# A hybrid encoder layer: a triangular substitution spread over the weight tiles, two projections exchanged, and one projection's sums in other PSUM banks

## The chip, the core and the metric

The kernel runs on one core of a Trainium2 chip. TensorE (PE) multiplies matrices and sums into PSUM banks of 128 partitions by 512 floats; VectorE (DVE), ScalarE (ACT) and GpSimd (POOL) do the rest, and SyncE (SP) issues most DMAs, some of which POOL issues too. Each engine works through its own list of instructions in order and waits where an instruction's operands or buffers aren't ready. The metric is the device time of one execution in microseconds (us), as the median of several runs.

## The reference

Two layers over 256 tokens of width 1024. Each layer normalises its input and feeds two mixers, whose outputs are gated, projected, merged and projected once more:

```python
h = rmsnorm(x, norm_w)
qa, ka, va, ab, za, qb, kb, vb, zb, ga, gb = split(h @ w_in)
# branch a: gated delta rule, chunks of 64, forward and backward
T = triangular_solve(I + L, I)            # L strictly lower, 64 x 64 for each head and chunk
u, w = T @ (v * beta), T @ (k * beta * exp(g))
ya = rmsnorm(o_fwd + o_bwd, gdn_norm_w) * silu(za)
# branch b: differential attention, 8 heads, two softmaxes per head
a = softmax(q0 @ k0.T) - lam * softmax(q1 @ k1.T)
yb = rmsnorm(a @ vb, subln_w) * (1 - lambda_init) * silu(zb)
# merge
x = x + (sigmoid(ga) * (ya @ w_pa) + sigmoid(gb) * (yb @ w_pb)) @ w_out
```

All inputs and the output are 32-bit floats; a final rmsnorm closes the trunk.

## The kernel before

A product of 32-bit precision is made of three matmuls: each operand is split into a high part and the rest, and high by high, high by low and low by high are summed in one bank. For the weights, SP loads a tile `raw` of two k-tiles (256 rows by 512 columns, a *weight pair*, three buffers), ACT casts it to `hi` (L248) and DVE subtracts to get `lo` (L250), two buffers of each. Twelve matmuls of 128x512 then use the pair: two k-tiles, two halves of the tokens, three products (L262 to L264). Their sums stand in two accumulators of a pool `ps_p` of four banks, which the next projection but one needs again. Smaller products use `ps_c` (two banks) and `ps_m` (two).

A layer goes through its projections in this order: the convolved q, k, v of branch a (`conv`) with q and k of branch b between (`qk_part`); `zb` and `za` in two halves each, with the eight heads' scores, softmaxes (`scores`) and value products (`attend`) woven in; the gates `gb`; `pb`, which multiplies the attention's output; the gates `ga`; `pa`; `o`. So zb0 means the first half of zb, of four weight pairs.

Beside them runs the triangular solve. `substitute` solves blocks of 32 by 32 on DVE, 31 rows, of which each takes a product (`fstmp`) and a subtraction (`X`). `spread_blocks` copies the result transposed (`lt`) and writes both to a DRAM tile `udr`; `merges(0)` and `merges(1)` read that back into `T64` tiles and `U_` (DMAs of POOL and SP) and join the blocks on PE to 64 (`y64p`) and 128 (`y128p`). `chunks(0)` and `chunks(1)` then apply the delta rule; the four products `ktm` by `kds` on DVE belong to them. Their result is scaled, turned (`pt_ya`) and split into `yaT`, which `pa` multiplies; `ybT`, from `pt_yb`, is the same for `pb`.

A scheduler sets each engine's list: it simulates the engines and takes the instructions by priority as they come ready. `tc.issue_after(x)`, here often as `behind(x)`, keeps an instruction behind x in the order, and `place(at)` names a matmul of a projection: `names[at // 8]`, k-tile `at % 8`, so that 32 to 39 is gb0. The steps of `merges` and `chunks` are pinned to such places. `mark[nm, kp]` holds cast and subtraction of weight pair kp.

The convolved v goes through DRAM to be turned (`bounce`, tile `tb_v`), and ACT scales it into `vtm` (L571). ACT also empties qk's accumulators into `stg` (L462).

Of the kernel before, what the change touches and what calls it, by code (L numbers as in the profile page):

```python
# [8 lines left out]
F32 = mybir.dt.float32  # L9
F32R = mybir.dt.float32r  # L10
I32 = mybir.dt.int32
AF = mybir.ActivationFunctionType
ALU = mybir.AluOpType
# [4 lines left out]
P = 128  # L18
# [3 lines left out]
NM = SEQ // P  # L22
# [6 lines left out]
HP = None  # L29
# [20 lines left out]
def hybrid_encoder(  # L50
# [31 lines left out]
    ps_c = pool("ps_c", 2, PSUM)  # L82
# [5 lines left out]

    def banks2(name):
        return [ps_p.tile([P, 512], F32, tag="p", name=f"{name}{i}") for i in range(2)]  # L90

    def bank_c(name):
        return ps_c.tile([P, 512], F32, tag="c", name=name)

    def mid(ap, n):
        return ap.unsqueeze(1).to_broadcast([ap.shape[0], n] + list(ap.shape[1:]))

    def last(ap, n):
        return ap.unsqueeze(ap.ndim).to_broadcast(list(ap.shape) + [n])

    mark = {}
# [119 lines left out]
    def behind(ins):  # L221
        return nullcontext() if ins is None else tc.issue_after(ins)
# [29 lines left out]
            for k in range(2):  # L252
                yield 2 * kp + k, hi[:, k, :n], lo[:, k, :n]

    def proj_tm(act, w, c0, n, evac, nm, places=(None,) * 4, spare=(), later=None, turned=(), between=None):

        accs = banks2(f"pp_{nm}")
        for kt, hi, lo in weights(w, c0, n, nm, places, later=later, spare=spare, turned=turned):
            for m in range(NM):
                ts_ = slice(m * P, (m + 1) * P)  # L260
                o = accs[m][:, :n]
                T.matmul(o, act[kt // 4][:, 0, kt % 4, ts_], hi, start=kt == 0, stop=False)  # L262
                T.matmul(o, act[kt // 4][:, 0, kt % 4, ts_], lo, start=False, stop=False)  # L263
                mark["proj"] = T.matmul(o, act[kt // 4][:, 1, kt % 4, ts_], hi, start=False,  # L264
                                        stop=kt == KT - 1).ins
                mark["done", nm, kt] = mark["proj"]
        if between:
            between()
        for m in range(NM):
            evac(m, accs[m][:, :n])  # L270
# [89 lines left out]
    for l in range(DEPTH):  # L360
# [175 lines left out]
        def conv(seg, c_base, slot, g):  # L536
            def evac_conv(acc, b0):
                vf = []
                for b in range(2):
                    j4 = b0 + b  # L540
                    cb = c_base // P + 4 * g + j4
                    ca = work.tile([P, SEQ], F32, tag="conv", name=f"cv{seg}{l}{g}{j4}", bufs=2)
                    S.activation(ca, acc[:, b, :], AF.Copy, scale=cw[:, 2, cb : cb + 1])  # L543
                    for j in (0, 1, 3, 4):
                        sft = j - 2
                        o0, o1 = max(0, -sft), SEQ - max(0, sft)
                        V.scalar_tensor_tensor(ca[:, o0:o1], acc[:, b, o0 + sft : o1 + sft],  # L547
                                               cw[:, j, cb : cb + 1], ca[:, o0:o1],
                                               ALU.mult, ALU.add)
                    if b == 0:  # L550
                        ths = work.tile([P, 2, SEQ], F32, tag="vf", name=f"th{seg}{l}{g}{j4}", bufs=2)
                    th = ths[:, b, :]
                    S.activation(th, ca, AF.Tanh, scale=0.5)
                    if slot is None:
                        f_ = th.rearrange("p (m t) -> p m t", m=NM)
                    else:
                        f_ = kq[:, 4 * g + j4, :, slot, :]
                    mark["conv"] = V.scalar_tensor_tensor(
                        f_, th.rearrange("p (m t) -> p m t", m=NM), 1.0,
                        ca.rearrange("p (m t) -> p m t", m=NM), ALU.add, ALU.mult).ins  # L560
                    vf.append(f_)
                if seg == "q":
                    return
                if seg == "v":
                    tb = squares(f"v{l}{g}{b0}")
                    turn_squares(tb, ths.rearrange("p b (m t) -> p (b m) t", m=NM))
                    bounce(tb, f"v{l}{g}{b0}")
                    for b in range(2):
                        for m in range(NM):
                            hd = 4 * g + b0 + b  # L570
                            S.activation(vtm[:, m, hd, :].rearrange("p (i d) -> p i d", i=4),  # L571
                                         tb[:, :, 2 * b + m, :], AF.Copy, scale=nrm[:, m, hd : hd + 1])
                    return
                pt = bank_c(f"ct{seg}{l}{g}{b0}")
                ptv = pt.rearrange("p (b m d) -> p b m d", b=2, m=NM)
                for b in range(2):
                    for m in range(NM):
                        T.transpose(ptv[:, b, m, :], vf[b][:, m, :], ident)
                bs = slice(4 * g + b0, 4 * g + b0 + 2)
                S.copy(ktm[:, :, bs, :].rearrange("p m b d -> p b m d"), ptv)  # L580
                for b in range(2):
                    for m in range(NM):
                        hd = 4 * g + b0 + b
                        S.activation(sqj[:, :P], ptv[:, b, m, :], AF.Square,
                                     accum_out=ssk[:, m, hd : hd + 1])
            proj_fm(hT, wl, c_base + 512 * g, evac_conv, f"{seg}{l}{g}",
                    turned=(3,) if (seg, g) == ("q", 1) else ())

        gdr = dram.tile([NM, 8, 2, P], F32, tag="gdr", name=f"gdr{l}")
        lnc = small.tile([P, 2, NM, NH], F32, tag="lnc", name=f"lnc{l}")  # L590
# [106 lines left out]
            with tc.issue_after(mark["conv"]):  # L697
                V.tensor_copy(la[64:P], lt[64:P].rearrange("p j i -> p i j"))

        def substitute(j0, j1):  # L700
            for j in range(j0, j1):
                ni, nr = 31 - j, j + 1
                tv = tmp[:, : nr * ni].rearrange("p (c i) -> p c i", c=nr)
                V.tensor_tensor(tv, mid(la[:, j, j + 1 :], nr), last(X[:, :nr, j], ni), ALU.mult)
                V.tensor_tensor(X[:, :nr, j + 1 :], X[:, :nr, j + 1 :], tv, ALU.subtract)

        def spread_blocks():
# [12 lines left out]
        def step(gens):  # L720

            for g_ in gens:
                next(g_)
# [86 lines left out]
        def chunks(g):  # L810
# [17 lines left out]
                S.copy(flat(y1[d]), ps)  # L828
            yield
            for d in range(2):  # L830
                with behind(mark["spread"]):
                    V.tensor_tensor(st[d], st[d], last(kds[:, d, hs4], P), ALU.mult)
                ps = four(f"sp{d}", lambda j: st[d][:, j, :], lambda j: y1[d][:, j, :])
                S.copy(flat(st[d]), ps)
# [52 lines left out]
        def scores(h, after):  # L887
            es = work.tile([P, 2, NM, SEQ], F32, tag="w4a", name=f"es{l}{h}", bufs=2)
            mx = small.tile([P, 2, NM], F32, tag="mx", name=f"mx{l}{h}")
            sp = [bank_c(f"sc{l}{h}{n}") for n in range(2)]  # L890
            for qt in range(NM):
                for n in (1, 0):
                    rows = slice(64 * n, 64 * n + 64)
# [45 lines left out]
        def z_part(z, c_base, nm, i):  # L939
            def evac_z(m, ps):  # L940
                silu2(z[i][:, m, :], ps)
            proj_tm(hT, wl, c_base + 512 * i, 512, evac_z, f"{nm}{l}{i}")


        if l == 0:
# [23 lines left out]
        conv("q", C_QA, 1, 1)  # L969
        take_blocks()  # L970
        qk_part(0, 1)
        substitute(0, 8)
        conv("v", C_VA, None, 0)
        qk_part(1, 0)
        substitute(8, 14)
        conv("v", C_VA, None, 1)
        qk_part(1, 1)
        substitute(14, 20)

        names = [f"{nm}{l}{i}" for nm in ("zb", "za", "gb", "pb", "ga") for i in range(2)]  # L980
        place = lambda at: mark["done", names[at // KT], at % KT]
        es = {}
        for p in range(4):
            z_part((zb, za)[p // 2], (C_ZB, C_ZA)[p // 2], ("zb", "za")[p // 2], p % 2)
            for h in (2 * p, 2 * p + 1):
                es[h] = scores(h, place(4 * h))
                if h:
                    attend(h - 1, es[h - 1], place(4 * h + 1), place(4 * h + 3))
            if p == 1:
                substitute(20, 31)  # L990
                spread_blocks()
                mg = [merges(0), merges(1)]
                step(mg)
                step(mg)
        def gated(o_, z_, r_, nw_, yT, nm, tiles=range(NM)):
            for i in range(2):
                for m in tiles:
# [35 lines left out]
        ybT = pair(f"ybT{l}")  # L1033
        gated(lambda i, m: heads4(ob[i][:, m, :]), zb, rb, nw[:, 1:2], ybT, f"yb{l}")

        branch(ybT, w_pb[l], gtb, f"pb{l}")
        gta = gate(C_GA, f"ga{l}", "eo")
        ch = [chunks(0), chunks(1)]

        def run(gen, at):  # L1040
# [1 line left out]
            with tc.high_priority(offset=HP):  # L1042
                next(gen, None)

        order = [(mg, 34), (mg[:1], 37), (mg[1:], 39), (mg, 42), (mg, 44)]
        order += [(ch[i : i + 1], at + i) for at in (48, 51, 54, 57, 60, 63, 66) for i in range(2)]
        for gens, at in order:
            if at == 48:
                key_sums()
            for gen in gens:  # L1050
                run(gen, at)
# [96 lines left out]
```

## Time and profile before

| | |
|---|---|
| median of three runs | 776.07 us (775.88 to 779.17) |
| profiled execution, its own time | 778.13 us |
| its span | 776.4 us |
| mean granted clock of TensorE | 0.994 |
| busy: PE, DVE, ACT, POOL | 752.7, 576.8, 471.7, 123.3 us |

The profile shows one execution, and its engine times are shares of its span. A row of a timeline is start, duration, engine, line, operation and its tiles (output<-input), and in brackets how long the engine was idle before and what ended that. A row of groups (with |) ends in the sum of busy time, the mean of one in ns, and the idle time before. A row of windows begins with the stretch and its length, then busy time and count of PE, PE's weight loads, DVE, ACT and POOL, the granted clock, the share of DMA time and GB/s. Buffer numbers are left out of names.

### The profile page before, as it was taken

The numbers are of one execution on the slowest core, as the hardware profiler recorded it, in microseconds if no ns is written. First come the engines' busy times: TensorE is split into PE (matmuls) and PEld (weight loads), VectorE is DVE, ScalarE is ACT, GpSimd is POOL, SyncE is SP. The second block draws the span as 40 slices with busy tenths as digits, with TensorE's granted clock in tenths as the row PEclk, the third lists the DMA queues.
The fourth block names the chain that finished last, engine by engine and source line by source line (L and its number), as shares of the span: only waits on it lengthen the run. The fifth ranks groups of instructions, "written<-read, shape, count | busy, mean of one in ns | idle before, by whom it ended". The sixth has DMA issues, their size and how long they took to land. (4 is left out here: it accounts for less than half of the span.)

```text
span 776.4 us, 13742 instructions
## 1 busy us (share of the span) xinstructions
PE 752.7 (97%) x5158; PEld 641.0 (83%) x5158; DVE 576.8 (74%) x1083; ACT 471.7 (61%) x1012; POOL 123.3 (16%) x187
## 2 busy tenths in 40 slices
PE   7999999989999999999999999999999998999996
PEld 4899889967778789888889889887777887998884
DVE  5686899989976735567677779999998575537682
ACT  6657675658776654565545678556687656456542
POOL 5000431111231020000010025202114012001000
PEclk9999999999999999999999999999999999999999
DMA  7752667755596523357674257767557862333641
GB/s 230 236 176 82 223 198 198 224 149 175 151 221 201 184 89 108 85 171 234 217 224 136 82 156 252 203 189 221 161 163 177 231 189 89 109 109 109 210 143 54
DMA packets 71794, 131.24 MB, mean 169 GB/s; under 512 B 12287, under 2 KB 12751, under 8 KB 71728
## 3 DMA queue, kind: packets, MB, share of 16 engines
q1 hardware_dynamic: 62718, 111.94, 48.3%
q0 software_dynamic: 6304, 15.15, 7.4%
q10 hardware_dynamic: 2706, 3.28, 1.2%
q8 instruction: 40, 0.66, 0.4%
q14 instruction: 26, 0.21, 0.1%
HBM read 123.44 MB, written 6.91 MB: 168 GB/s over the span
## 5 line engine op out<-in xcount | busy, mean ns | idle before, releaser
L263 PE MATMUL pp_qk<-lo_qk,hT 128*128 128x512 f32 x128 | 51.0, 399 | 0.8 <-DVE lo_qk L250 0.5
L264 PE MATMUL pp_qk<-hi_qk,hT 128*128 128x512 f32 x128 | 50.0, 391 | 0.0
L250 DVE TENSOR_TENSOR lo_qk<-raw_qk,hi_qk 128x1024 fp32r<-128x1024 f32 x32 | 39.7, 1242 | 9.8 <-ACT hi_qk L248 9.5
L262 PE MATMUL pp_qk<-hi_qk,hT 128*128 128x512 f32 x128 | 45.2, 393 | 0.0
L250 DVE TENSOR_TENSOR lo_pb<-raw_pb,hi_pb 128x1024 fp32r<-128x1024 f32 x16 | 19.6, 1224 | 32.4 <-ACT hi_pb L248 32.4
L904 ACT ACTIVATE es<-sc,mx 128x256 f32<-128x256 f32 x64 | 29.7, 476 | 21.4 <-DVE mx L902 21.4
L248 ACT CAST hi_qk<-raw_qk 128x1024 fp32r<-128x1024 f32 x28 | 29.4, 1049 | 20.4 <-PE pp_qk L264 10.6
L320 PE MATMUL pf_q<-hT,hi_q 128*128 128x256 f32 x128 | 36.2, 286 | 0.0
L318 PE MATMUL pf_q<-hT,hi_q 128*128 128x256 f32 x128 | 36.1, 287 | 0.0
L318 PE MATMUL pf_v<-hT,hi_v 128*128 128x256 f32 x128 | 35.9, 285 | 0.0
L318 PE MATMUL pf_k<-hT,hi_k 128*128 128x256 f32 x128 | 35.8, 285 | 0.0
L320 PE MATMUL pf_v<-hT,hi_v 128*128 128x256 f32 x128 | 35.8, 284 | 0.0
L320 PE MATMUL pf_k<-hT,hi_k 128*128 128x256 f32 x128 | 35.7, 283 | 0.0
L322 PE MATMUL pf_q<-hT,lo_q 128*128 128x256 f32 x128 | 34.8, 285 | 0.0
L322 PE MATMUL pf_v<-hT,lo_v 128*128 128x256 f32 x128 | 34.5, 288 | 0.0
L322 PE MATMUL pf_k<-hT,lo_k 128*128 128x256 f32 x128 | 34.3, 283 | 0.0
L250 DVE TENSOR_TENSOR lo_ga<-raw_ga,hi_ga 128x1024 fp32r<-128x1024 f32 x16 | 19.6, 1224 | 16.5 <-ACT hi_ga L248 16.5
L262 PE MATMUL pp_pb<-hi_pb,ybT 128*128 128x512 f32 x64 | 27.6, 432 | 4.3 <-ACT ybT L215 4.3
L250 DVE TENSOR_TENSOR lo_gb<-raw_gb,hi_gb 128x1024 fp32r<-128x1024 f32 x16 | 19.5, 1217 | 16.0 <-ACT hi_gb L248 16.0
L547 DVE SCALAR_TENSOR_TENSOR cvq<-pf_q,cw,cvq 128x254 f32<-128x254 f32 (+1 forms) x64 | 29.8, 476 | 1.9 <-ACT cvq L543 1.4
L263 PEld LDWEIGHTS pp_qk<-lo_qk,hT 128*128 128x128 f32 x128 | 24.0, 188 | 8.1 <-DVE lo_qk L250 3.1
L250 DVE TENSOR_TENSOR lo_pa<-raw_pa,hi_pa 128x1024 fp32r<-128x1024 f32 x16 | 19.6, 1223 | 14.8 <-ACT hi_pa L248 14.8
(362 smaller groups left out, 2529.6 us busy)
## 6 DMA issues: line engine op xcount, KB each, us to landing
raw_qk<-in_w_in_dram SPq DMA_DIRECT2D x32, 512.0 KB, 3.9
raw_k<-in_w_in_dram SPq DMA_DIRECT2D x16, 512.0 KB, 4.8
raw_q<-in_w_in_dram SPq DMA_DIRECT2D x16, 512.0 KB, 3.7
raw_v<-in_w_in_dram SPq DMA_DIRECT2D x16, 512.0 KB, 4.0
raw_zb<-in_w_in_dram SPq DMA_DIRECT2D x16, 512.0 KB, 3.8
raw_za<-in_w_in_dram SPq DMA_DIRECT2D x16, 512.0 KB, 3.8
raw_gb<-in_w_in_dram SPq DMA_DIRECT2D x16, 512.0 KB, 6.2
raw_o<-in_w_out_dram SPq DMA_DIRECT2D x16, 512.0 KB, 5.0
```

The lines of the kernel that those rows point to most:

```text
L248: high = (V.tensor_copy if kp in turned else S.copy)(hi[:, :, :n], raw[:, :, :n]).ins
L250: mark[nm, kp] = high, V.tensor_tensor(lo[:, :, :n], raw[:, :, :n], hi[:, :, :n].bitcast(F32), ALU.subtract).ins
L262: T.matmul(o, act[kt // 4][:, 0, kt % 4, ts_], hi, start=kt == 0, stop=False)
L263: T.matmul(o, act[kt // 4][:, 0, kt % 4, ts_], lo, start=False, stop=False)
L264: mark["proj"] = T.matmul(o, act[kt // 4][:, 1, kt % 4, ts_], hi, start=False, stop=kt == KT - 1).ins
L318: T.matmul(o, hi[:, cs], act[kt // 4][:, 0, kt % 4, :], start=first, stop=False, skip_group_check=True)
L320: T.matmul(o, hi[:, cs], act[kt // 4][:, 1, kt % 4, :], start=False, stop=False, skip_group_check=True)
L322: T.matmul(o, lo[:, cs], act[kt // 4][:, 0, kt % 4, :], start=False, stop=done, skip_group_check=True)
L547: V.scalar_tensor_tensor(ca[:, o0:o1], acc[:, b, o0 + sft : o1 + sft], cw[:, j, cb : cb + 1], ca[:, o0:o1], ALU.mult, ALU.add)
L904: S.activation(es[:, n, qt, :], spv[:, qt, :], AF.Exp, bias=mx[:, n, qt : qt + 1], accum_out=s_all[:, h, n, qt : qt + 1])
```

## The change

It does five things; no instruction is added to or taken from the computation.

1. The rows of the substitution stood in blocks (rows 0 to 7, 8 to 13, 14 to 19, 20 to 30) at points of the program. Now `pace` lists the weight pairs from the second qk projection to za's last but one or two, with z pairs twice, `cost` estimates each row, and row j comes behind the `lo` of pair `due[j]`.
2. The scaling of v into `vtm` is taken out of `conv` and put behind four named casts (`place_v`).
3. The first projection, zb0, sums in the two `ps_c` banks; the scores of heads 0 and 1 use `ps_p` in exchange, those of the later heads two `ps_c` banks as before.
4. `ga` is projected before `pb`, and the steps of `merges` and `chunks` move to later places.
5. The `ktm` products come behind the second `lo` of gb1 and not behind the transposed copy `lt`.

```diff
+    def banks2_c(name):
+        return [ps_c.tile([P, 512], F32, tag="c", name=f"{name}{i}") for i in range(2)]
...
-        accs = banks2(f"pp_{nm}")
+        accs = (banks or banks2)(f"pp_{nm}")
...
-                    for b in range(2):
-                        for m in range(NM):
-                            hd = 4 * g + b0 + b
-                            S.activation(vtm[:, m, hd, :].rearrange("p (i d) -> p i d", i=4),
-                                         tb[:, :, 2 * b + m, :], AF.Copy, scale=nrm[:, m, hd : hd + 1])
+                    loose.append((tb, 4 * g + b0))
                     return
...
+        def place_v(after):
+
+            tb, h0 = loose.pop(0)
+            for b in range(2):
+                for m in range(NM):
+                    hd = h0 + b
+                    with behind(after):
+                        S.activation(vtm[:, m, hd, :].rearrange("p (i d) -> p i d", i=4),
+                                     tb[:, :, 2 * b + m, :], AF.Copy, scale=nrm[:, m, hd : hd + 1])
...
-        def substitute(j0, j1):
-            for j in range(j0, j1):
+        pace = [f"qk{l}10", f"v{l}1", f"qk{l}11", *(f"{nm}{l}{i}" for nm in ("zb", "za") for i in range(2))]
+        pace = [(nm, kp) for nm in pace for kp in range(4) for _ in range(1 + (nm[0] == "z"))][:-2]
+        cost = [2 * (60 + (31 - j) * (j + 1)) for j in range(31)]
+        due = [pace[len(pace) * sum(cost[:j]) // sum(cost)] for j in range(31)]
+
+        def substitute(nm):
+            for j in [j for j in range(31) if due[j][0] == nm]:
                 ni, nr = 31 - j, j + 1
                 tv = tmp[:, : nr * ni].rearrange("p (c i) -> p c i", c=nr)
-                V.tensor_tensor(tv, mid(la[:, j, j + 1 :], nr), last(X[:, :nr, j], ni), ALU.mult)
+                with behind(mark[due[j]][1]):
+                    V.tensor_tensor(tv, mid(la[:, j, j + 1 :], nr), last(X[:, :nr, j], ni), ALU.mult)
...
-                with behind(mark["spread"]):
+                with behind(mark[f"gb{l}1", 1][1]):
                     V.tensor_tensor(st[d], st[d], last(kds[:, d, hs4], P), ALU.mult)
...
-            sp = [bank_c(f"sc{l}{h}{n}") for n in range(2)]
+            sp = (banks2 if h < 2 else banks2_c)(f"sc{l}{h}")
...
-            proj_tm(hT, wl, c_base + 512 * i, 512, evac_z, f"{nm}{l}{i}")
+            proj_tm(hT, wl, c_base + 512 * i, 512, evac_z, f"{nm}{l}{i}",
+                    banks=None if i or nm == "za" else banks2_c)
...
-        substitute(0, 8)
         conv("v", C_VA, None, 0)
         qk_part(1, 0)
-        substitute(8, 14)
+        substitute(f"qk{l}10")
         conv("v", C_VA, None, 1)
+        substitute(f"v{l}1")
         qk_part(1, 1)
-        substitute(14, 20)
-
-        names = [f"{nm}{l}{i}" for nm in ("zb", "za", "gb", "pb", "ga") for i in range(2)]
+        substitute(f"qk{l}11")
+        place_v(mark[f"qk{l}11", 3][0])
+
+        names = [f"{nm}{l}{i}" for nm in ("zb", "za", "gb", "ga", "pb") for i in range(2)]
...
-            if p == 1:
-                substitute(20, 31)
-                spread_blocks()
-                mg = [merges(0), merges(1)]
-                step(mg)
-                step(mg)
+            substitute(names[p])
+            if p == 0:
+                place_v(mark[f"zb{l}0", 0][0])
+                place_v(mark[f"zb{l}0", 3][0])
+            elif p == 1:
+                place_v(mark[f"zb{l}1", 1][0])
+        with tc.high_priority(offset=HP):
+            spread_blocks()
+        mg = [merges(0), merges(1)]
+        step(mg)
+        step(mg)
...
+        gta = gate(C_GA, f"ga{l}", "eo")
         branch(ybT, w_pb[l], gtb, f"pb{l}")
-        gta = gate(C_GA, f"ga{l}", "eo")
...
-        order = [(mg, 34), (mg[:1], 37), (mg[1:], 39), (mg, 42), (mg, 44)]
-        order += [(ch[i : i + 1], at + i) for at in (48, 51, 54, 57, 60, 63, 66) for i in range(2)]
+        order = [(mg, 39), (mg[:1], 42), (mg[1:], 44), (mg, 47), (mg, 49)]
+        order += [(ch[i : i + 1], at + i) for at in (52, 54, 57, 59, 62, 64, 67) for i in range(2)]
         for gens, at in order:
-            if at == 48:
+            if at == 52:
```

How the lists change is shown at three places, in the first layer. First PE where zb0 begins, before: `pp_qk` is the accumulator of the last qk projection, `pp_zb000` and `pp_zb001` are zb0's two, `sc` the scores of head 0.

```order
L264 MATMUL pp_qk0111_1914<-hi_qk0113_1969,hT0_1_108 128x512
L262 MATMUL pp_zb000_2025<-hi_zb000_2027,hT0_0_107 128x512
L263 MATMUL pp_zb000_2025<-lo_zb000_2028,hT0_0_107 128x512
L264 MATMUL pp_zb000_2025<-hi_zb000_2027,hT0_0_107 128x512
L262 MATMUL pp_zb000_2025<-hi_zb000_2027,hT0_0_107 128x512
L263 MATMUL pp_zb000_2025<-lo_zb000_2028,hT0_0_107 128x512
L264 MATMUL pp_zb000_2025<-hi_zb000_2027,hT0_0_107 128x512
L262 MATMUL pp_zb000_2025<-hi_zb001_2045,hT0_0_107 128x512
L262 MATMUL pp_zb001_2026<-hi_zb000_2027,hT0_0_107 128x512
L263 MATMUL pp_zb001_2026<-lo_zb000_2028,hT0_0_107 128x512
L264 MATMUL pp_zb001_2026<-hi_zb000_2027,hT0_0_107 128x512
L895 MATMUL sc001_2106<-qkT0_0_281 128x256
```

After, from the second matmul of zb0 on:

```order
L266 MATMUL pp_zb001_1996<-hi_zb000_1997,hT0_0_107 128x512
L267 MATMUL pp_zb000_1995<-lo_zb000_1998,hT0_0_107 128x512
L268 MATMUL pp_zb000_1995<-hi_zb000_1997,hT0_0_107 128x512
L267 MATMUL pp_zb001_1996<-lo_zb000_1998,hT0_0_107 128x512
L268 MATMUL pp_zb001_1996<-hi_zb000_1997,hT0_0_107 128x512
L266 MATMUL pp_zb000_1995<-hi_zb000_1997,hT0_0_107 128x512
L267 MATMUL pp_zb000_1995<-lo_zb000_1998,hT0_0_107 128x512
L268 MATMUL pp_zb000_1995<-hi_zb000_1997,hT0_0_107 128x512
L266 MATMUL pp_zb001_1996<-hi_zb000_1997,hT0_0_107 128x512
L267 MATMUL pp_zb001_1996<-lo_zb000_1998,hT0_0_107 128x512
L268 MATMUL pp_zb001_1996<-hi_zb000_1997,hT0_0_107 128x512
L913 MATMUL sc001_2076<-qkT0_0_281 128x256
```

The two accumulators are now used in turn from the start, and the first score matmul comes behind all twelve of the first pair and not behind ten matmuls.

Next PE at the end of gb1, before: `pt_yb` are the transposes of the attention's output, and `pp_pb` needs `ybT`.

```order
L262 MATMUL pp_gb_2733<-hi_gb_2788,hT_1_108 128x512
L263 MATMUL pp_gb_2733<-lo_gb_2789,hT_1_108 128x512
L264 MATMUL pp_gb_2733<-hi_gb_2788,hT_1_108 128x512
L206 MATMUL pt_yb_2847<-ident,ob_0_352 128x128
L206 MATMUL pt_yb_2858<-ident,ob_0_352 128x128 x4
L262 MATMUL pp_pb_2887<-hi_pb_2889,ybT_0_2841 128x512
L263 MATMUL pp_pb_2887<-lo_pb_2890,ybT_0_2841 128x512
L262 MATMUL pp_pb_2888<-hi_pb_2889,ybT_0_2841 128x512
L263 MATMUL pp_pb_2888<-lo_pb_2890,ybT_0_2841 128x512
```

After:

```order
L812 MATMUL y128p_3394<-T_2628,A_339 64x64
L812 MATMUL y128p_3375<-T_2621,A_339 64x64
L812 MATMUL y128p_3394<-T_2628,A_339 64x64
L209 MATMUL pt_yb_2880<-ident,ob_1_353 128x128 x3
L266 MATMUL pp_ga_2887<-hi_ga_2889,hT_0_107 128x512
L267 MATMUL pp_ga_2887<-lo_ga_2890,hT_0_107 128x512
L268 MATMUL pp_ga_2887<-hi_ga_2889,hT_0_107 128x512
L266 MATMUL pp_ga_2888<-hi_ga_2889,hT_0_107 128x512
L267 MATMUL pp_ga_2888<-lo_ga_2890,hT_0_107 128x512
```

Matmuls of the merge (`y128p`) and the transposes now stand before `pp_ga`, which needs only `hT`; pb follows eight weight pairs later.

Last POOL's DMAs from `udr`, before:

```order
L735 MEMSET T_2336 32x8x32
L736 MEMSET T_2336 32x8x32
L712 DMA udr_343<-X_346 8x8x1024 x2
L712 DMA udr_343<-lt_345 8x8x1024 x2
L739 DMA T_2329<-udr_343 32x16x32 x4
L743 DMA U__96<-udr_343 32x32x32 x4
L153 TENSOR_SCALAR rspre<-ssb_351 128x16
L154 TENSOR_TENSOR rb_2834<-rspre,mhalf 128x16
```

After:

```order
L730 DMA udr_343<-X_346 8x8x1024 x2
L730 DMA udr_343<-lt_345 8x8x1024 x2
L761 DMA U__96<-udr_343 32x32x32 x4
L753 MEMSET T_2621 32x8x32
L754 MEMSET T_2621 32x8x32
L757 DMA T_2621<-udr_343 32x16x32 x4
L753 MEMSET T_2628 32x8x32
L754 MEMSET T_2628 32x8x32
L156 TENSOR_SCALAR rspre<-ssb_351 128x16
L157 TENSOR_TENSOR rb_2834<-rspre,mhalf 128x16
```

The copies into `U_` now come ahead of T's memsets and DMAs, and both pairs of memsets come behind `udr`. On SP the four DMAs of the other T tile move from ahead of gb0's first load to behind its fourth. On DVE the last row of X now stands ahead of za1's last `lo`, where it stood ahead of za1's first; the `ktm` products go from behind the copy `lt` to between the second and third `lo` of gb1, with two products into `B` (L673) behind them.

More of the change, by code (lines that the diff above doesn't have):

```diff
@@ L253, in weights, with proj_tm @@
                 yield 2 * kp + k, hi[:, k, :n], lo[:, k, :n]
-    def proj_tm(act, w, c0, n, evac, nm, places=(None,) * 4, spare=(), later=None, turned=(), between=None):
-        accs = banks2(f"pp_{nm}")
+    def proj_tm(act, w, c0, n, evac, nm, places=(None,) * 4, spare=(), later=None, turned=(), between=None,
+                banks=None):
+        accs = (banks or banks2)(f"pp_{nm}")
         for kt, hi, lo in weights(w, c0, n, nm, places, later=later, spare=spare, turned=turned):
@@ L587, in conv @@
                     turned=(3,) if (seg, g) == ("q", 1) else ())
+        loose = []
+        def place_v(after):
[6 more added lines that the diff above has]
+                                     tb[:, :, 2 * b + m, :], AF.Copy, scale=nrm[:, m, hd : hd + 1])
         gdr = dram.tile([NM, 8, 2, P], F32, tag="gdr", name=f"gdr{l}")
```

## The prediction

> **What bounds the kernel now.** First the page's busy line, then what PE waited for, since an engine in use for almost the whole span is the bound and only its waits can be won back.
>
> ```profile
> span 776.4 us, 13742 instructions
> PE 752.7 (97%) x5158; PEld 641.0 (83%) x5158; DVE 576.8 (74%) x1083; ACT 471.7 (61%) x1012; POOL 123.3 (16%) x187
> PE pp_pb L262 <- ACT ybT L215: 4.3, 2, 2.3
> PE pp_zb L262 <- ACT stg L462: 3.8, 2, 2.5
> PE pp_za L262 <- ACT hi_za L248: 1.3, 2, 0.6
> PE pp_zb L263 <- DVE lo_zb L250: 0.8, 2, 0.6
> ```
>
> PE is busy 752.7 of 776.4 us, and its work isn't changed. Each wait (total, times, longest) comes twice, once per layer. The first two are on the change's path. Next, the timeline of ACT and PE where the first layer's z projections begin.
>
> ```profile
> 163.39 1.28 ACT L571 ACTIVATE vtm<-tb_v,nrm 128x128 f32<-128x128 f32 x4 [1.99 <-DMA tb_v<-bnc_v]
> 164.58 0.56 ACT L462 COPY stg<-pp_qk 128x512 f32<-128x512 f32 x1
> 165.04 1.05 ACT L248 CAST hi_zb<-raw_zb 128x1024 fp32r<-128x1024 f32 x1
> 161.12 0.40 PE L262 MATMUL pp_qk<-hi_qk,hT 128*128 128x512 f32 x1
> 162.26 0.39 PE L264 MATMUL pp_qk<-hi_qk,hT 128*128 128x512 f32 x1
> 165.19 0.50 PE L262 MATMUL pp_zb<-hi_zb,hT 128*128 128x512 f32 x1 [2.54 <-ACT stg L462]
> 543.29 0.50 PE L262 MATMUL pp_zb<-hi_zb,hT 128*128 128x512 f32 x1 [1.25 <-ACT stg L462]
> ```
>
> ACT stands at the vtm scaling until a DMA brings tb_v; behind it waits the copy that empties a bank of the last qk projection, and PE needs that bank for zb. From 161.12 to 162.26 lie five matmul steps: 0.228 us each, 2.74 us for the twelve of a weight pair.
>
> The other stalls end at ybT, and two of the four are followed by a slower clock. In the windows the seventh value after the stretch's length is the granted clock.
>
> ```profile
> 269.96 0.71 PE L206 MATMUL pt_yb<-ident,ob 128*128 128x128 f32 x5
> 272.98 0.50 PE L262 MATMUL pp_pb<-hi_pb,ybT 128*128 128x512 f32 x1 [2.31 <-ACT ybT L215]
> 649.52 0.50 PE L262 MATMUL pp_pb<-hi_pb,ybT 128*128 128x512 f32 x1 [2.01 <-ACT ybT L215]
> 163.00:166.00 3.00, 0.81 (x4) 0.68 (x5) 2.10 (x8) 2.61 (x7) 0.00 (x0) 1.00 0.64 189
> 166.20:169.60 3.40, 3.40 (x11) 2.21 (x11) 2.71 (x7) 0.76 (x2) 0.00 (x0) 0.50 0.26 36
> 272.00:276.00 4.00, 3.02 (x15) 2.34 (x16) 2.94 (x4) 2.19 (x4) 2.19 (x4) 1.00 0.41 133
> 543.00:547.00 4.00, 3.71 (x19) 2.64 (x20) 4.00 (x12) 2.09 (x4) 0.00 (x0) 1.00 0.46 131
> 651.00:654.30 3.30, 3.30 (x10) 2.64 (x9) 0.75 (x1) 0.69 (x1) 1.16 (x3) 0.50 0.49 168
> ```
>
> After the idle stretches of 2.54 and 2.01 us the clock stands at 0.50 for about 3.4 us; after those of 2.31 and 1.25 us it doesn't. Half a clock for 3.4 us costs 1.7 us, twice: 3.4 us.
>
> **The change, part by part.** *Removed.* With zb's first sums in the two c banks, PE no longer waits for stg: 2.54 + 1.25 = 3.8 us. With ga ahead of pb, eight weight pairs, 8 × 2.74 = 22 us of ga, stand between the transposes pt_yb and the first pb matmul, and ybT, 2.31 us late before, has all that time: 4.3 us off. No idle stretch of 2 us is then left to set off a half clock: 3.4 us off. The lo_zb waits, 0.8 us, lie in the stretch that is paced anew; I take them off here and put their successors on below. Sum: 3.8 + 4.3 + 3.4 + 0.8 = 12.3 us. The hi_za waits I leave in.
>
> The Trainium skill (TensorE: Matmul & The Clock Gate, "Why this matters for your kernels") says that idle gaps up to about 3 us don't bring the half clock, and by it none of the 3.4 us hangs on these waits. The trace shows one after a gap of 2.01 us, none after two others; I go by the rows, and the rule is a rival below.
>
> *Added, first at zb.* The next rows are the ones that price it.
>
> ```profile
> L902 DVE TENSOR_REDUCE mx<-sc 128x2 f32<-128x512 f32 x32 | 21.4, 684 | 3.7 <-PE sc L895 3.6
> L904 ACT ACTIVATE es<-sc,mx 128x256 f32<-128x256 f32 x64 | 29.7, 476 | 21.4 <-DVE mx L902 21.4
> L904 ACT ACTIVATION_READ_ACCUMULATOR es<-sc,mx 128x1 f32 x64 | 13.1, 204 | 0.0
> L832 DVE TENSOR_TENSOR ktm<-ktm,kds 128x512 f32<-128x512 f32 x8 | 5.0, 693 | 0.0
> L673 DVE TENSOR_TENSOR B<-kq,B 128x1024 f32<-128x1024 f32 x8 | 9.7, 1218 | 1.1 <-PE kq L641 1.1
> 160.00:240.00 80.00, 76.57 (x511) 58.80 (x510) 68.84 (x147) 57.02 (x156) 14.41 (x24) 0.98 0.66 177
> ```
>
> (a) The vtm scaling, stg and the second hi_zb stay in this order on ACT. That cast ended at 165.04 + 1.05 = 166.1. PE, starting zb at 162.5, is through the first pair at 165.2 and a score matmul later at 165.4: 0.7 us idle in the first layer. In the second it starts at 543.29 − 1.25 = 542.0 and is done at 544.8, past the cast's end: nothing. (b) The second projection zb needs the p bank in which head 1's scores were, free only after a maximum (0.68) and the exponentials with their accumulator reads (2 × 0.68): at most 2.0 us if PE comes at once, nothing if its own zb matmuls cover it. In the new order twelve of them cover most; walking the queues with these durations leaves 0.85 us, my value. (c) DVE is busy 68.84 of 80 us here. Rows of the substitution that stood in blocks now stand one or two behind each lo; the total is the same and nothing excludes a gain. I keep 0.4 us per layer, what lo_zb cost before; the ends are 0 and the 0.6 us of its longest wait.
>
> *Added at gb.* (d) The four ktm products move from the za stretch to between the second and the third lo of gb1, where two B products follow: 4 × 0.62 + 2 × 1.22 = 4.9 us against a weight pair's 2.74. Two lo tiles are held ahead, so not all of it shows; I count 0.4 us, with 0 and the whole ktm block, 2.5 us, as ends. Queued behind are the last two lo of gb1.
>
> *Moved at the end.* The steps of chunks run one place later against the k-tiles, half a pair or 1.37 us.
>
> ```profile
> 718.98 1.41 DVE L216 SCALAR_TENSOR_TENSOR yaT<-pt_ya,nw,yaT 128x512 fp32r<-128x512 f32 x2
> 722.92 0.61 PE L262 MATMUL pp_pa<-hi_pa,yaT 128*128 128x512 f32 x2
> ```
>
> yaT was ready at 720.39, 2.5 us ahead of pa; about 1.2 us of that stays. Now it is lo_pb that shares DVE with this chain: (e) 0.5 us per layer, between 0 and 0.8. Exchanging ga and pb moves no matmul off or onto PE, and their loads are the same on SP.
>
> *Sum.* (a) 0.7; (b) to (e) 0.85 + 0.4 + 0.4 + 0.5 = 2.15 per layer, 4.3 for two: 5.0 us back on. The profiled execution took 778.13 us (1.7 around its span): 778.13 − 12.3 + 5.0 = 770.8. The median, 776.07, lies 2.1 below; the runs go from 775.88 to 779.17, 3.3 us, the size of two half-clock stretches. I take it that the median run had one fewer, so that only 10.6 us come off it: 776.07 − 10.6 + 5.0 = **770.5 us**. Without any of the added waits it is 765.5; half way to the upper ends of (b) to (e), 7.5 us off together, it is 774.
>
> **The rivals.** *The waits are replaced (0.17).* PE is so dense that each buffer is just in time. With (b) and (d) at their upper ends, 2 × 2.0 and 2 × 2.5, and (a), (c), (e) at 0.7, 0.8, 1.0, 11.5 us come on: 777.0 us. Where the waits of 2 us bring half clocks again, 1.7 each, it ends at 780.4. For it speaks the DVE row; against it, that PE loses only 0.8 us to lo_zb in that row's stretch.
>
> *The triangular blocks come late: slower (0.15).* In place, PE's y64p matmuls of merges, which read the T blocks.
>
> ```profile
> 211.12 0.30 POOL L735 MEMSET T<- 32x256 f32 x1 [13.46 <-DVE fstmp L704]
> 211.48 0.31 POOL L736 MEMSET T<- 32x256 f32 x1
> 212.08 1.52 POOL L712 DMA_DIRECT2D udr<-X  x2 [0.30 <-DVE X L705]
> 213.60 1.10 POOL L712 DMA_DIRECT2D udr<-lt  x2
> 219.21 2.60 POOL L739 DMA_DIRECT2D T<-udr  x4 [4.51 <-issue]
> 221.80 3.11 POOL L743 DMA_DIRECT2D U__96<-udr  x4
> 218.72 2.31 SPq L739 DMA_DIRECT2D T<-udr  x4
> raw_gb<-in_w_in_dram SPq DMA_DIRECT2D x16, 512.0 KB, 6.2
> L757 PE MATMUL y64p<-T,A x256: 191/191/212, 238.4 to 616.5; 32*32 32x32 f32 x128
> DMA to landing us min/median/max: 3.8/5.0/8.3
> DMA to landing us min/median/max: 3.8/5.0/7.3
> ```
>
> (The last two rows are of udr and of T.) Before, T was issued by 221.81, landed 5.0 later at 226.8, and was read at 238.4: 11.6 us to spare. Now the U copies, 3.11 us, go first on POOL, and the two memsets, 0.30 and 0.31, stand between: 3.7 us in all. The last row of X stands only behind the last lo but one of za1, and from there PE has two pairs of za1 and four of gb0, 6 × 2.74 = 16.4 us, and some 4 us of the last heads' scores and transposes, my estimate from the walk: 20.5 us to y64p, where it had 238.4 − (212.08 − 0.30) = 26.6. To spare: 11.6 − 3.7 − 6.1 = 1.8 us. With the slowest landings, 3.3 + 2.3 us more, y64p is 3.8 us late; with DVE a weight pair behind, 6.5 us, and the pause would bring a half clock, 1.7: 16.4 us in two layers, 786.9 us. It decides above 4.7 us per layer, which takes 770.5 past 779.95. Median landings speak against it. On SP, the other group's T (218.72, 2.31 us) moves behind the fourth load of gb0, and gb1's loads queue behind it: held until udr lands, 7.1 us after X as before (212.08 to 219.21), and 2.31 more, then 6.2 to land, they are there some 16 us after X, and PE wants gb1 only after y64p, at 20.5.
>
> The Trainium skill (DMA: Bandwidth & Descriptors, "Anatomy of one DMA — SWDGE (gpsimd) path") gives 2.0 us plus the bytes at 436 GB/s, for a T block of 64 KB an estimated 2.15 us; the two landings would leave 5.7 us more to spare and this rival no chance. The rows show 5.0, and I keep it.
>
> *The half clocks come anyway (0.08).* If what throttles doesn't hang on these gaps, as the skill's rule has it, 1.7 or 3.4 us stay on: 772.2 to 773.9 us. Against it: both stretches began within 4 us of a gap.
>
> **How the numbers follow.** The forecast has 0.60; its own range is 765.5 to 774, and 0.08 of it lies above 772.2. The bounds are 0.5% of 776.07, 3.9 us, about what a measurement of this kernel can tell from no change: 772.2 and 779.95. Faster: 0.52 + half of the last rival, 0.04: 0.56. Same: 0.08 + 0.04 + 0.13 of the first rival = 0.25. Slower: 0.15 + the 0.04 of the first rival with its half clocks = 0.19. From 764.5 (a gain at the paced DVE stretch, a microsecond) to 779.5 the range holds all but the second rival and the first's tail.
>
> **What would show it.** In the changed profile the waits of pp_zb for stg and of pp_pb for ybT must be gone, and no stretch after 10 us have a clock of 0.50. New: pp_zb for hi_zb once, for es or mx about 0.9 us twice; gb's second projection for lo about 0.4. A wait of y64p for T over 2 us, or pp_pa for yaT, would make the prediction wrong; so would lo_zb and lo_za waits of more than 3 us together, the pacing having made DVE the bound.

## The result, and the profile after

The changed kernel takes 772.40 us, the median of 18 runs (770.51 to 775.43), against 777.56 us for the kernel before in the same sessions (18 runs, 774.14 to 781.17). The ratio is 0.9941, with a 95% interval of 0.9929 to 0.9952: 4.6 us faster by the ratio, 5.2 between the medians, where 5.6 were forecast. The time is in the range; how it comes about isn't what the prediction said. One execution among all that follow, of the fifth experiment, took 922.89 us at a mean granted clock of 0.755, and no figure here counts it.

First the busy line of the changed kernel's page and what PE waited for there (total, times, longest).

```profile
span 773.7 us, 13772 instructions
PE 756.6 (98%) x5158; PEld 643.9 (83%) x5158; DVE 577.7 (75%) x1083; ACT 471.9 (61%) x1012; POOL 125.9 (16%) x187
PE wb_n L165 <- POOL tri L116: 3.1, 1, 3.1
PE pp_gb L267 <- DVE lo_gb L253: 1.9, 4, 0.7
PE sc L913 <- ACT stg L466: 0.5, 1, 0.5
PE pp_zb L266 <- ACT hi_zb L251: 0.5, 2, 0.2
```

Every wait that was to go has gone: pp_pb for ybT (4.3), pp_zb for stg (3.8), pp_zb for lo_zb (0.8), and also pp_za for hi_za (1.3), which the prediction left in. Yet PE's busy time, which no part of the change was to touch, rose from 752.7 to 756.6 us. The stretches where the clock was 0.50 before show that it isn't the clock, which is the sixth value after the length (the prediction's text counts it as the seventh):

```profile
166.00:170.00 4.00, 3.75 (x18) 2.40 (x17) 4.00 (x10) 2.22 (x4) 0.00 (x0) 1.00 0.22 32
640.00:660.00 20.00, 20.00 (x213) 17.15 (x211) 11.95 (x15) 15.23 (x26) 0.64 (x1) 1.00 0.46 144
```

So PE lost 3.4 us of half clock and gained 3.9 us of busy time. The groups of PE show where: first the scores of before, then those of the changed kernel, and one head's matmuls in the two timelines (before at 184.61, the changed kernel at 194.05 and 195.76).

```profile
L895 PE MATMUL sc<-qkT 64*128 64x256 f32 x128 | 19.8, 409 | 0.0
184.61 1.13 PE L895 MATMUL sc<-qkT 64*128 64x256 f32 x8
```

```profile
L913 PE MATMUL sc<-qkT 64*128 64x256 f32 x128 | 27.8, 413 | 0.5 <-ACT stg L466 0.5
194.05 0.70 PE L913 MATMUL sc<-qkT 64*128 64x256 f32 x2
194.68 1.16 PE L946 MATMUL av<-vb,aT 128*128 128x128 f32 x8
195.76 1.13 PE L913 MATMUL sc<-qkT 64*128 64x256 f32 x6
```

The same 128 score records take 27.8 us and not 19.8. A head's four score matmuls (eight records) use one half and the other of the array's 128 rows in turn, and where two on different halves stand side by side their records overlap: eight records in 1.13 us. In the changed kernel the first stands alone, two records in 0.70 us, and the other six still take 1.13. In PE's list of before, one head of eight in each layer is split so; in the new list, seven: twelve more splits of 0.70 us are 8.4.

The two profiled executions add up. Off: 4.3 + 3.8 + 0.8 + 1.3 of waits and 3.4 of half clock, 13.6 us. On: 8.0 of scores, 1.9 + 0.5 + 0.5 of waits, 10.9. That is 2.7 us, and 778.13 − 775.43 is 2.7. Smaller rows that the sum leaves out move too (the `at` transposes take 11.1 us and not 9.6, the waits of pp_vb for hT 1.9 and not 0.9), so the agreement to a tenth is partly chance. The profiled execution of the changed kernel is the slowest of its 18, 3.0 us above their median; what the others had less of, no profile shows.

### The profile page after: what moved, and what is told of

It reads as the page before. It is cut to its first block, busy times and chain, and to the rows that moved or that the text cites. A ratio compares the mean times of both kernels' runs of the same rounds, so it can differ in the third digit from the quotient of the medians.

```text
span 773.7 us, 13772 instructions
## 1 busy us (share of the span) xinstructions
PE 756.6 (98%) x5158; PEld 643.9 (83%) x5158; DVE 577.7 (75%) x1083; ACT 471.9 (61%) x1012; POOL 125.9 (16%) x187
## 4 chain that ended last, share of the span: by engine, by line
PE 75%; DVE 10%; DMA 9%; ACT 3%; issue 2%; POOL 1%; SPq 0%; POOLq 0%; DVEq 0%; ACTq 0%
PE pp_vb L306 4%; PE sc L913 3%; DMA raw_gb<-in_w_in_dram 2%; PE pp_qk L267 2%; PE pp_qk L268 2%; DMA raw_vb<-in_w_in_dram 2%; PE pp_qk L266 2%; PE pp_o L306 2%; PE pf_v L322 2%; PE pp_za L267 2%; PE pf_v L326 2%; PE pf_v L324 2%; PE pp_ga L268 2%; PE pp_ga L266 2%; PE pf_k L322 2%
## 5 line engine op out<-in xcount | busy, mean ns | idle before, releaser
L251 ACT CAST hi_pa<-raw_pa 128x1024 fp32r<-128x1024 f32 x16 | 16.9, 1054 | 23.2 <-PE pp_pa L268 17.0
L551 DVE SCALAR_TENSOR_TENSOR cvv<-pf_v,cw,cvv 128x254 f32<-128x254 f32 (+1 forms) x64 | 30.0, 480 | 0.1
L551 DVE SCALAR_TENSOR_TENSOR cvk<-pf_k,cw,cvk 128x254 f32<-128x254 f32 (+1 forms) x64 | 28.5, 479 | 2.0 <-ACT cvk L547 1.3
L253 DVE TENSOR_TENSOR lo_ga<-raw_ga,hi_ga 128x1024 fp32r<-128x1024 f32 x16 | 19.4, 1223 | 12.7 <-ACT hi_ga L251 12.7
```

What stands on the lines that cost most here:

```text
L251: high = (V.tensor_copy if kp in turned else S.copy)(hi[:, :, :n], raw[:, :, :n]).ins
L253: mark[nm, kp] = high, V.tensor_tensor(lo[:, :, :n], raw[:, :, :n], hi[:, :, :n].bitcast(F32), ALU.subtract).ins
```

## The experiments

All ratios are against the kernel before, on the same chip in the same session, with 95% intervals. x1 to x10 below stand for the ten experiments in their order.

**The bank exchange alone.** To the kernel before:

```diff
+            sp = (banks2 if h < 2 else banks2_c)(f"sc{l}{h}")
...
+                    banks=None if i or nm == "za" else banks2_c)
```

> The kernel before with the third part of the change alone: zb0 sums in the two c banks, heads 0 and 1 score in p banks. Theory (split scores): with this alone the four score matmuls of a head no longer stand together in PE's list in six more heads of each layer, so the 64 score records of a layer take about 13 us where they took 9.1 to 9.4; the zb wait for stg (3.8 us) and a half clock (1.7) go, the ybT waits (4.3) stay; 7.5 on and 5.5 off: 1.000 to 1.005 of before. Rival (the split costs nothing, the loss comes of the paced rows): score records stay at 9.2 us a layer and the time is about 0.993 of before.

Measured: 1.0017 (1.0005 to 1.0030), 779.00 us.

```profile
L898 PE MATMUL sc<-qkT 64*128 64x256 f32 x128 | 26.4, 412 | 0.2 <-ACT stg L465 0.2
PE pp_pb L265 <- ACT ybT L218: 1.2, 2, 0.6
```

As the theory has it, the exchange by itself splits the scores (+6.6 us of records) and gives nothing. Two parts were not foreseen, and they offset each other. The ybT wait fell to 1.2 us by itself and no half clock is left. And other small matmuls take longer as well: in the profile `at` goes from 9.6 to 11.7 us, `av` from 17.2 to 19.4, `kq` from 8.4 to 10.2. So the time of this run isn't a measure of the score splits alone.

**The bank exchange undone.** In the changed kernel:

```diff
-            sp = (banks2 if h < 2 else banks2_c)(f"sc{l}{h}")
+            sp = banks2_c(f"sc{l}{h}")
...
-                    banks=None if i or nm == "za" else banks2_c)
+                    banks=None)
```

> The changed kernel with the third part undone: zb0 sums in p banks, all scores in c banks. Theory (split scores): score records back to about 9.2 us a layer and av to 6.6, together 9.4 us less over two layers than in the changed kernel; the waits of zb for stg come back (3.8) and perhaps a half clock (1.7): about 0.989 of before. Rival (the split costs nothing): the change loses its zb part, about 1.001 of before.

Measured: 0.9998 (0.9975 to 1.0021), 777.33 us: the theory's time is wrong, though its scores are right.

```profile
L913 PE MATMUL sc<-qkT 64*128 64x256 f32 x128 | 18.2, 402 | 0.0
PE pp_zb L266 <- ACT stg L466: 3.7, 2, 2.1
PE pp_gb L266 <- ACT hi_gb L251: 2.9, 2, 1.6
PE pp_gb L267 <- DVE lo_gb L253: 2.0, 4, 0.5
```

The score records fell by 9.6 us (those of `av`, expected to fall too, stay at 17.2), the stg wait came back, and a new wait stands at gb, 2.9 us for its casts. With more pauses on PE the mean granted clock of the 12 runs is 0.9932 where the changed kernel's 18 have 0.9973; 0.0041 of 776 us is 3.2 us. That isn't the whole account. The profiled execution took 774.20 us, 3.1 below the median of its 12 (772.02 to 781.60), and the changed kernel's lies 3.0 above its own, so the rows of these two profiles don't explain why the median is 0.0057, some 4.4 us, above the changed kernel's. The part beyond the clock stays open.

**The vtm scaling one cast later, banks as before.** To the kernel just shown:

```diff
-                place_v(mark[f"zb{l}0", 0][0])
+                place_v(mark[f"zb{l}0", 1][0])
```

> As the run before it, and the second vtm scaling placed one cast later on ACT, behind the two stg copies. Theory (the stall at zb is one of ACT's order, not of the banks): the wait of zb for stg goes without the bank exchange, 3.8 us and a half clock less, 2 heads of 8 have split scores, 2.5 us more: about 0.985 of before. Rival (stg is late for another reason, the last qk matmuls): the wait stays above 1 us in each layer and the time at 0.989 or above.

Measured: 0.9916 (0.9896 to 0.9935), 771.72 us; no wait for stg is left, so the stall was one of ACT's order. The gain is smaller than expected (0.985): zb now waits 1.9 us for lo_zb, gb 1.5 for lo_gb. The time falls on the rival's side, its cause doesn't.

**The split alone.** In the kernel before, the first score matmul keeps its place and the others are pinned one k-tile later:

```diff
-                    with behind(None if qt or not n else after), tc.high_priority(offset=HP):
+                    with behind(after[qt + 1 - n > 0]), tc.high_priority(offset=HP):
...
-                es[h] = scores(h, place(4 * h))
+                es[h] = scores(h, (place(4 * h), place(4 * h + 1)))
```

> The kernel before, with the first score matmul of a head kept at its place and the other three pinned one k-tile later, so that six more heads of each layer have split scores; nothing else is edited. Theory (split scores): 0.63 us for each of 12 heads, score records about 13 us a layer, 7.5 us in all: 1.008 to 1.010 of before. Rival (a lone score matmul costs nothing that the projections don't give back): score records 9.2 us a layer, 0.998 to 1.002.

Measured: 1.0098 (1.0072 to 1.0123), 784.78 us.

```profile
L895 PE MATMUL sc<-qkT 64*128 64x256 f32 x128 | 28.3, 415 | 0.0
PE pp_pb L262 <- ACT ybT L215: 4.3, 2, 2.3
PE pp_zb L262 <- ACT stg L462: 3.8, 2, 2.5
```

8.5 us more of score records, 7.6 us more time (0.0098 of 777.7), and the two large waits as before; those for hi_za (1.3) and lo_zb (0.8) are gone, while `av` and `at` take 0.7 and 0.5 us more. From a lone score to the next matmul the timeline of before has 0.63 us (192.94 to 193.57), and twelve times that is 7.6. So a split costs about its full PE time, and this is the run that settles the theory.

**The exchange of ga and pb alone**, with the changed places of merges and chunks, in the kernel before:

```diff
-        branch(ybT, w_pb[l], gtb, f"pb{l}")
         gta = gate(C_GA, f"ga{l}", "eo")
+        branch(ybT, w_pb[l], gtb, f"pb{l}")
...
```

> The kernel before with the fourth part alone: ga projected ahead of pb, and the steps of merges and chunks at the changed places. Theory (each stall is worth its idle time and the half clock behind it): the ybT waits, 4.3 us, and the half clock after pb go, the stg waits at zb (3.8) stay, scores stay together (9.1 to 9.4 us a layer): 0.993 to 0.995 of before, mean granted clock about 0.996. Rival (the gain is given back at the other end, where pa waits for yaT): pp_pa waits 1 us or more in each layer, 0.997 to 1.000.

Measured: 0.9892 (0.9876 to 0.9907), 769.50 us in three runs: better than the whole change, and than expected.

```profile
L895 PE MATMUL sc<-qkT 64*128 64x256 f32 x128 | 19.5, 404 | 0.0
PE pp_zb L262 <- ACT stg L462: 3.9, 2, 2.6
PE pp_za L262 <- ACT hi_za L248: 1.4, 2, 0.7
160.00:180.00 20.00, 17.15 (x83) 12.65 (x82) 18.67 (x48) 12.10 (x29) 2.74 (x5) 1.00 0.58 172
```

Scores and zb are as before, ybT and yaT are not waited for. The mean granted clock is 0.9983; the kernel before, run beside it, has 0.9945 on average: 0.0038 of 776, 2.9 us, and with the 4.3 of ybT 7.2 of the 8.4 us. The rest isn't assigned. The idle stretch at zb is still 2.6 us, and no half clock follows it here.

**The changed kernel without the pacing**, with blocks and merges called as before:

```diff
-            substitute(names[p])
...
+                substitute(20, 31)
+                spread_blocks()
+                mg = [merges(0), merges(1)]
```

> The changed kernel with the substitution in its old blocks and merges called where they were; the banks, the exchange of ga and pb, the vtm and ktm places stay. Theory (the gain comes of banks and exchange, the pacing adds little): score records 12.5 to 13.2 us a layer, no lo_zb or hi_za wait over 1 us in a layer, 0.993 to 0.996 of before. Rival (without pacing DVE is late for lo): waits for lo_zb, lo_za or hi_za of 3 us or more together, 0.997 to 1.000.

Measured: 0.9909 (0.9897 to 0.9922), 770.82 us: without the pacing the change is about 2.5 us faster, and faster than forecast. Past the start PE's longest wait is 0.4 us; the scores still take 27.8 us. The waits of ACT and POOL's rows show what pacing does, first in the changed kernel, then without.

```profile
ACT hi_gb L251 <- DMA raw_gb<-in_w_in_dram: 9.8, 4, 3.9
221.36 1.26 POOL L730 DMA_DIRECT2D udr<-X  x2 [25.89 <-issue]
228.93 1.97 SPq L757 DMA_DIRECT2D T<-udr  x4
237.95 10.24 SPq L247 DMA_DIRECT2D raw_gb<-in_w_in_dram  x3
```

```profile
ACT hi_gb L251 <- DMA raw_gb<-in_w_in_dram: 5.0, 2, 3.0
212.81 1.16 POOL L725 DMA_DIRECT2D udr<-X  x2
221.63 1.41 SPq L752 DMA_DIRECT2D T<-udr  x3
239.31 7.03 SPq L247 DMA_DIRECT2D raw_gb<-in_w_in_dram  x3
```

Pacing ends the substitution 8.5 us later, at 221.4 instead of 212.8, and the udr, T and U copies move with it. The last three loads of gb's weights are then issued until 248.2 and not 246.3, ACT waits 9.8 us in all for gb's weights and not 5.0, and PE waits 1.9 us for lo_gb, none without. That it is the copies that hold up the loads is a reading of these rows; no run tests it alone.

**The ktm products later**, in the kernel of the third experiment:

```diff
-                with behind(mark[f"gb{l}1", 1][1]):
+                with behind(mark[f"gb{l}1", 3][1]):
```

> The kernel of x3_no_bank_v_late with the ktm products behind gb1's last lo and not behind its second. Theory (the ktm block is what delays gb1's third lo): pp_gb's wait for lo falls from 1.5 to below 0.5 us and the time by about 1 us against that kernel, to 0.990 of before. Rival (the loads of gb1 or the two B products delay it): the wait stays at 1.2 or more, time as x3.

Measured: 0.9897 (0.9878 to 0.9917), 769.50 us. The wait for lo_gb went from 1.5 to 1.2 us only, the rival's side; the times of the two kernels have overlapping intervals. Inconclusive on the time; the ktm block isn't what gb mainly waits for.

**No pacing, banks as before, vtm later.** The third experiment's kernel with the sixth's edit.

> The kernel of x3_no_bank_v_late with the substitution in its old blocks: banks as before, vtm one cast later, ga ahead of pb, ktm in gb1. Theory (pacing adds little, as above; 3 of 8 heads split in the list): score records about 10 us a layer, 0.990 to 0.994 of before. Rival (pacing carries part of the gain): lo_zb, lo_za, hi_za waits of 3 us or more, 0.995 or above.

Measured: 0.9875 (0.9858 to 0.9893), 767.69 us, the lowest ratio here and below the forecast, though the intervals of the fifth, seventh and ninth experiments overlap with it. It is some 3 us less than x3, with pacing. The score records take 22.3 us (20 were expected), and the waits of gb are gone; 1.9 us for lo_zb are left. Beside the sixth experiment, from which it differs by the banks and one vtm place, it is 2.6 us faster (0.9875 and 0.9909): moving that cast does more than the bank exchange does.

**The exchange, and only one vtm scaling moved.** To the fifth experiment's kernel:

```diff
+                    if (g, b0) == (0, 2):
+                        loose.append((tb, 4 * g + b0))
+                        return
...
+            if p == 0:
+                place_v(mark[f"zb{l}0", 1][0])
```

> The kernel of x5_swap_only with one more edit: the vtm scaling of the second v tile is placed behind the second cast of zb0, so that both stg copies stand ahead of it on ACT; banks, substitution and ktm as before. Theory (the stall at zb is one of ACT's order): the stg waits of 3.9 us go, one head of eight in each layer stays split as before (score records 9.1 us), lo_zb may wait up to 2 us in all as in x3 and x8: 0.985 to 0.987 of before. Rival (DVE then limits zb, so that the gain is given back as lo_zb waits): lo_zb and hi_za waits of 4 us or more, 0.989 or above.

Measured: 0.9882 (0.9863 to 0.9900), 768.78 us: of the 3.9 us of stg waits at most about 1 arrives, and the interval overlaps with the fifth experiment's. DVE takes part of the rest, in the rival's direction, but its waits stay below the rival's 4 us:

```profile
PE pp_zb L263 <- DVE lo_zb L250: 1.9, 2, 1.0
PE pp_za L263 <- DVE lo_za L250: 1.7, 2, 0.8
```

**Scores kept together by later pins.** To the eighth experiment's kernel:

```diff
-                es[h] = scores(h, place(4 * h))
+                es[h] = scores(h, place(4 * h + (2 if h in (5, 6) else 1 if h == 3 else 0)))
```

> The kernel of x8_x3_no_pace with the scores of heads 3, 5 and 6 pinned one or two k-tiles later, so that the four matmuls of a head stand together for seven heads of eight instead of five; nothing else is edited. Theory (split scores, 0.63 us a head): score records fall from 10.4 to about 9.1 us a layer, 2.5 us off: 0.984 to 0.985 of before. Rival (later scores delay the softmax chain by as much): waits for aT or es of 2 us or more, 0.987 or above.

Measured: 0.9954 (0.9937 to 0.9971), 774.06 us: 6 us lost. The rival was right:

```profile
L908 PE MATMUL sc<-qkT 64*128 64x256 f32 x128 | 21.3, 436 | 0.0
PE at L934 <- DVE es L923: 4.8, 2, 2.5
```

PE waits 4.8 us for a softmax whose scores came late, and half clocks follow those waits (0.50 from 219.46 to 222.88 and from 594.93 to 601.76); the mean granted clock fell to 0.993. The records fell by 1.0 us of the 2.5 expected, but two heads stand in half-clock stretches and take 1.98 and 2.08 us where 1.13 is usual. Without that the fall is 2.8 us: the theory has the records right, and the delay costs more than they give.

## Why the prediction was right, and where it was wrong

**The waits that go: right.** The stg and ybT waits are gone with the values of the sum, 3.8 and 4.3. That the first was worth a bank exchange was wrong: x3 removes it by ACT's order alone.

**The half clock: right in size.** The kernel before has a mean granted clock of 0.992 to 0.997 in 23 runs (mean 0.9944) and a span of 778.3 us at the low end, 773.2 at the high one; the changed kernel has 0.996 to 0.998 (mean 0.9973). The difference is 0.0029 of 776, 2.3 us, between the 1.7 that the forecast took off the median and the 3.4 of the profile. The rival in which half clocks come anyway has fallen: from 13.5 us on, the changed kernel's profile has no stretch at 0.50 but the last 2.4 us, when PE is done. The Trainium skill (TensorE: Matmul & The Clock Gate, "Why this matters for your kernels") has no such stretch after gaps under about 3 us; here they went with gaps of 2.0 to 2.5 us. Still, x5 keeps a gap of 2.6 us and has none. What decides it can be read from the twelve profiles, of the two kernels and the ten experiments. Inside one profile the half-clock stretches start whole multiples of 3.413 us apart (166.18 and 650.87 in the kernel before, 142 steps). Here are windows cut on that grid, from the kernel before and then, counted back from the half clock that begins at 764.62 and at 656.24, from x5 and x4.

```profile
162.76:166.18 3.42, 0.99 (x4) 0.85 (x5) 2.52 (x9) 2.79 (x7) 0.00 (x0) 1.00 0.62 190
166.18:169.59 3.41, 3.41 (x11) 2.20 (x12) 2.73 (x7) 0.78 (x2) 0.00 (x0) 0.50 0.25 35
268.57:271.99 3.42, 2.10 (x12) 1.54 (x10) 1.22 (x3) 3.37 (x7) 0.65 (x1) 1.00 0.39 145
271.99:275.40 3.41, 2.42 (x12) 1.87 (x13) 2.44 (x3) 2.15 (x4) 1.98 (x4) 1.00 0.31 95
647.45:650.87 3.42, 1.41 (x7) 0.94 (x7) 2.55 (x4) 2.59 (x5) 1.56 (x3) 1.00 0.07 19
650.87:654.28 3.41, 3.41 (x11) 2.77 (x10) 0.85 (x2) 0.69 (x1) 1.29 (x3) 0.50 0.48 165
```

```profile
163.88:167.29 3.41, 1.58 (x7) 1.31 (x8) 2.08 (x7) 3.38 (x8) 0.00 (x0) 1.00 0.53 158
167.29:170.70 3.41, 3.41 (x19) 2.37 (x18) 3.41 (x10) 0.56 (x2) 0.00 (x0) 1.00 0.41 101
161.31:164.72 3.41, 1.47 (x7) 0.89 (x5) 2.71 (x6) 1.49 (x6) 0.00 (x0) 1.00 0.68 206
164.72:168.14 3.42, 2.85 (x12) 2.09 (x12) 2.88 (x8) 2.34 (x5) 0.00 (x0) 1.00 0.24 91
```

PE's idle time is the length less its busy time. A window with 2.43 or 2.01 us idle is followed by half clock; one with 1.32 (before), 1.83 (x5) or 1.94 (x4) isn't. In the twelve profiles, cut so from 20 us on, every window with 2.0 us or more is followed by half clock, and no other window at full clock is; one stretch, in x10, lasts two windows. The gap in x5 falls on a boundary, 0.74 and 1.84 us, and the one before pb in the first layer of the kernel before does too. So in these runs a gap of 2.0 to 2.6 us brought a half clock or not by where it fell on the grid, whose place in the span differs between the profiles; the forecast's sum had the size right without knowing this.

**"PE's work isn't changed": wrong, and the largest term of all.** The prediction held PE's busy time fixed, since no matmul was added. But a score matmul costs by its neighbour: 8.0 us came on, against 5.0 for everything that was listed. The records of x1, x2 and x4 show it from three sides: with the exchange alone 26.4 us, without it 18.2, and split on purpose 28.3; x4 shows it in the time too, 7.6 us. The changed order was there to be read, but the two lists shown under The change both end at `sc001`, so they don't tell whether the other scores stand beside it or a projection does. The Trainium skill (the same page, "Part 3: Packing small matmuls — row/col tiling") says that matmuls on different rows of the array overlap, with starts some 4 ns apart. The trace agrees: the records of a pair start 6 or 7 ns apart in both kernels.

**Why the list splits** is argued, and the runs only bound it: in the new list the first score matmul waits for one of the two banks and the second for the other, which an earlier head's exponentials or zb's evacuation free later. The split comes with the bank exchange (x1) and goes without it (x2); two heads of eight are split in x3 and three in x8, which have no exchange, so it isn't the only cause. Pinning the scores later isn't a cure (x10).

**The added waits, term by term.** (a) 0.7 us at hi_zb: 0.5, and 0.5 for stg in front of a score. (b) 1.7 us for the bank of head 1's scores: no such wait. (c) 0.8 us of lo_zb: none, and hi_za's 1.3 us went as well. (d) 0.8 us at gb: 1.9, with another cause: not the ktm block (x7) but gb's late weights; the wait goes when the pacing does, though the ktm block stays (x6). (e) 1.0 us at pa: none. Together 5.0 were forecast and 2.9 measured. On the session's median of before, 777.56, the terms as measured (4.3, 3.8, 0.8, 1.3 and 2.3 of half clock off, 2.9 and the scores' 8.0 on) give 776.0 us; 772.4 were measured. Of these 3.6 us, 3.0 are the distance of the profiled execution from its median, and no run shows what they are. So that the time fell in the range is in part luck: a term of 8.0 put at nothing was met by added waits that stayed small, by hi_za, and by a part that stays open.

**The rivals.** Replaced waits at (b) and (d): 777 us, not seen; what replaced the waits was matmul time. The triangular blocks late: y64p isn't among the waits. T's last issue on POOL ended at 235.75 (233.17 and 2.58) and y64p began at 247.0, 11 us later.

```profile
T<-udr POOLq DMA_DIRECT2D x8, 64.0 KB, 8.6
```

The median landing took 8.6 us here, where the walk had 5.0; in exchange PE came to y64p 25.7 us after the last row of X (221.36 to 247.0), where the walk had 20.5. By the median some 3 us were to spare, not far from the walk's 1.8, because two terms that were too short offset each other.

## What to carry to other kernels

Where a matmul uses half of the array's rows, as the scores do here, its price is that of its neighbourhood: read the list for which matmuls stand side by side, not only for what waits. Undo each part of a bundled change alone: here one part (ga ahead of pb) was worth 8.4 us, and two others, the banks alone (x1) and the pacing (x6), cost 1.3 and 2.5 us, close to half of it. Part effects needn't add up: undoing the banks in the changed kernel made it slower (x2), and with one cast moved it didn't (x3). A stall named for a bank can be one of the order on the engine that empties the bank.

## What the runs showed of the hardware

The step from a 128-row projection matmul to a score and back is longer than within projections, 0.32 and 0.31 us against 0.23 in the records of both kernels, so in these records each extra switch has a price of its own. The granted clock differs between executions of one kernel: 0.992 to 0.997 in 23 runs of before, with about 0.8 us of span to each 0.001. In the twelve profiles, a half clock followed each full-clock window of 3.41 us on the grid above in which PE was idle for 2.01 us or more, and none in which it was idle for 1.94 or less.
